# A two-layer diffusion trunk: the adaLN sums' start as a step of its own, their steps placed anew, and raw output weights loaded earlier

## The chip, the cores and the metric

One core of a Trainium2 chip. The metric is the device time of one execution, in microseconds (us). Five engines work at the same time, each through its own list of instructions in order: TensorE (PE, matmuls), VectorE (DVE), ScalarE (ACT), GpSimd (POOL) and SyncE (SP), which here only issues DMA transfers. POOL and ACT issue some DMAs too.

## What is computed

A trunk of two layers over 512 latent tokens and 256 context tokens of width 1024, all in float32. Cut to what matters:

```python
mod_lat = (silu_c @ ada_w[i] + ada_b[i])          # adaLN: 6 vectors of 1024
sh1, sc1, g1, sh2, sc2, g2 = jnp.split(mod_lat, 6, axis=-1)
h_lat = modulate(rmsnorm(x, norm_g[i, 0]), sh1, sc1)
y_lat = hybrid_na_sgu(...) if i % 2 == 0 else retention_mixer(...)
x = x + g1 * rmsnorm(y_lat, norm_g[i, 1])
h = modulate(rmsnorm(x, norm_g[i, 2]), sh2, sc2)
x = x + g2 * rmsnorm(conv_ffn(h, ...), norm_g[i, 3])
```

The same is done for the context tokens with their own vectors, except behind the retention of layer 1, whose output for the context isn't needed. Layer 0 mixes with neighbourhood attention beside spatial gating, layer 1 with retention in 8 heads. Both have a gated MLP (the ffn) of width 2816 with a depthwise convolution.

## The kernel before, in words

**Stages.** Spatial gating (until about 158 us), attention of layer 0 (until about 330), the first ffn (turns until about 890), retention (975 to 1445), the second ffn (1470 to 1850). Every float32 matmul is made of three: weights and data are split into a high and a low part. `split` (L110) lets ACT write the high part and DVE the low one. Raw weights come through `load` (L97), which issues on SP's queue, into one of only three buffers of the tag "raw" (512 KB each). These three serve ffn_in (f00.., f10..), ffn_out (fo..) and the adaLN weights (ar..). A smaller buffer ("rawu") takes the other half of ffn_in (f01.., f11..).

**The adaLN vectors.** `setup` makes four of layer 0's twelve half vectors at the start; each of the others is made by a generator, `ada_half` (L251), for half a vector of 512. It clears an accumulator `acc` for each stream with a memset on POOL (L257) and writes the bias into its first row by DMA (L258 in the code; the row is issued on POOL where `side` is set, otherwise on SP through `load`). Then it loads the weights in four parts and adds them up on DVE, 4 (two streams) or 2 operations for a part; each is an `acc<-ar,cs,acc` of 128x512. After each part it yields. At the end acc is split (ah, al). For gates (halves 4, 5, 10, 11) a matmul with ones sums over the partitions (ag), and the product with a row of norm_g is written (ngr, then G); for the last two of layer 0 it goes to DRAM (`away`, g<-ngr). For shifts and scales a matmul with `sel` (ac), a copy (arow) and a transpose (at) bring the sums into columns. There is one acc for each stream: the next half's memset waits for the split of the half before.

**Where the steps go.** `self.jobs` holds the generators that a stage has to finish, and `bg(n)` (L238) runs the next n steps of the first one; `bg_all` runs what is left. The calls of bg stand between the pieces of the main work: three among the projections of attention's first pair and one in every second turn of its loop of 42 (L872 and after); four held together in retention's head 0 and four in each later head (L1391 and after); one to four in each turn of an ffn (L1703 and after). Operations pass a scheduler that orders each engine's instructions by expected readiness, except those issued while `hold` is set, which keep the program's order. So a moved call moves what is near it too.

**Around the change.** Attention splits its keys (ka, kb) into halves of the partitions; kb's upper half is copied by POOL (L970). POOL also makes the bias tiles from a slab that it loads and scales (L991 to L1005). In an ffn each turn j has products of features with weights of turn j (wa, wb, wc, wd, split from f00 and f01), takes of PSUM into `pre`, and pieces of the output product of earlier pairs (wf), whose results go to yp or ypg and from there to DRAM by POOL's accumulating DMAs (L1688). `w_out` (L1653) loads and splits one ffn_out row block; it is called once a turn. The last two turns' features have their own end (`out_last`).

Of the kernel before, what the change touches and what calls it, by code (L numbers as in the profile page):

```python
# [13 lines left out]
ALU = mybir.AluOpType  # L14
AX = mybir.AxisListType

P = 128
# [7 lines left out]
NF = 22  # L25
# [53 lines left out]
class Trunk:  # L79
# [170 lines left out]

    def ada_half(self, l, half, streams, gate=None, away=False, fine=False, side=False):  # L251
        S, V, T, G = self.S, self.V, self.T, self.G
        m, h = divmod(half, 2)
        acc = []
        for s in range(streams):
            t = (self.lp if s else self.bp).tile([P, 512], F32, name=f"acc{l}{half}{s}", tag=f"acc{s}", bufs=1)
            G.memset(t, 0.0)  # L257
            (G.dma_start if side else self.load)(t[0:1], self.a["adab_row"][l * 12 + half : l * 12 + half + 1])  # L258
            acc.append(t)
        for kp in range(4):  # L260
            raw = self.bp.tile([P, 1024], F32, name=f"ar{l}{half}{kp}", tag="raw", bufs=3)
            self.load(raw, self.ada_unit_src(l, half, kp))
            for kk in range(2):
                k = kp * 2 + kk
                for s in range(streams):
                    V.scalar_tensor_tensor(
                        out=acc[s],
                        in0=raw[:, kk * 512 : kk * 512 + 512],
                        scalar=self.cs[:, 8 * s + k : 8 * s + k + 1],
                        in1=acc[s],  # L270
                        op0=ALU.mult,
                        op1=ALU.add,
                    )
                if fine and kk == 0:
                    yield
            yield
        sp = []
        for s in range(streams):
            hi = self.t2k(f"ah{l}{half}{s}", F32R)
            lo = self.t2k(f"al{l}{half}{s}", F32R)  # L280
            self.split(hi, lo, acc[s])
            sp.append((hi, lo))
            if fine:
                yield
            if m in (2, 5):
                ps = self.ps(f"ag{l}{half}{s}", "C")
                T.matmul(ps, self.ones, hi, start=True, stop=False)
                T.matmul(ps, self.ones, lo, start=False, stop=True)
                ngr = self.t2k(f"ngr{l}{half}{s}")
                row = l * 4 + (1 if m == 2 else 3)  # L290
                src = self.a["norm_g"][row : row + 1, h * 512 : h * 512 + 512].broadcast_to([P, 512])
                (G.dma_start if side else self.load)(ngr, src)
                dst = gate[s][:, h * 512 : h * 512 + 512]
                if away:
                    V.tensor_tensor(out=ngr, in0=ps, in1=ngr, op=ALU.mult)
                    G.dma_start(dst, ngr)
                else:
                    V.tensor_tensor(out=dst, in0=ps, in1=ngr, op=ALU.mult)
        if m in (2, 5):
            return  # L300
        ps = self.ps(f"ac{l}{half}", "C")
# [11 lines left out]
        for s in range(streams):  # L313
            if m in (0, 3):
                V.tensor_copy(ab[:, s, 1, h * 4 : h * 4 + 4], pt[:, :, s])
            else:
                V.scalar_tensor_tensor(
                    out=ab[:, s, 0, h * 4 : h * 4 + 4],
                    in0=pt[:, :, s],
# [538 lines left out]
    def attention(self, y, final):  # L858
        a = self.a
        with ExitStack() as ctx:  # L860
# [13 lines left out]
            fills = self.project_pair(0, pairs[0])  # L874
            for i, f in enumerate(fills):
                f()
                if i in (0, 2, 4):
                    self.bg()
            self.take_qk(0, pairs[0])
            fills = self.project_pair(1, pairs[1])  # L880
            toks = (4, 5, 0, 1, 2, 3)
            for i in range(n + lag):
# [26 lines left out]
                if i < n and step == 3:  # L909
                    self.take_v(j, pr)  # L910
                if i % 2:
                    self.bg()
            self.bg_all()
            for f in fills:
# [200 lines left out]
    def retention(self, y, final):  # L1115
        S, V, T, G, a = self.S, self.V, self.T, self.G, self.a
        KS = float(np.float32(P) ** np.float32(-0.5))
        with ExitStack() as ctx:
# [231 lines left out]
            for h in range(8):  # L1350
                vg_tiles(h)
                if h == 0:
# [15 lines left out]
                    for half in range(2):  # L1368
# [6 lines left out]
                        for n in (range(4) if half else (2, 0, 1, 3)):  # L1375
# [10 lines left out]
                            if half and n == 2:  # L1386
# [3 lines left out]
                                states(h)  # L1390
                    V.hold = True  # L1391
                    self.bg(4)
                    V.hold = False
                else:
# [15 lines left out]
                    for tp in (2, 0, 1):  # L1410
                        nat(h, wv, tp, "v")
                        if tp < 2:
                            score(h, tp)
                    self.bg()
                    wg = vg(h, 16, "g")
# [3 lines left out]
                    self.bg()  # L1419
                if h < 7:  # L1420
                    wk = qk(h + 1, 8, "k")
                else:
                    self.turn += 3
                    o6 = f, w_out(6)
                    self.bg_all()
# [13 lines left out]
    def ffn(self, l, y, final, gates=None):  # L1439
# [13 lines left out]
        with ExitStack() as ctx:  # L1453
# [37 lines left out]
            def raw(src, name, up=False):  # L1491
                if up:
                    t = fp.tile([P, 1024], F32, name=f"{name}r", tag="rawu", bufs=1)
                else:
                    t = self.bp.tile([P, 1024], F32, name=f"{name}r", tag="raw", bufs=3)
                self.load(t, src)
                return t
# [154 lines left out]

            def w_out(f, kind="o"):  # L1653
                u = slot(kind, f"fo{l}{f}", 0)
                r = (l * NF + f) * P
                self.split(u[0], u[1], raw(a["ffn_out"][r : r + P], f"fo{l}{f}"))
                return u
# [37 lines left out]
            def o(i):  # L1695
                for _ in range(per[i]):
                    if pieces:
                        pieces.pop(0)()
# [4 lines left out]
            for j in range(2, NF):  # L1703
# [5 lines left out]
                group = j // 2 * 2 - 2  # L1709
                feats = [gs.get(group + i) for i in range(GF)]  # L1710
                product(X, d[11], hb(11), "only")
                product(Y, d["s", 2], hb(("t", 1)), "only")
# [12 lines left out]
                step()  # L1725
                o(1)
                if j % 2 == 0 and group < LAST:
                    wo = nwo + [w_out(group + 1)]
                    pieces += out_steps(feats, wo, group)
# [6 lines left out]
                if j % 2 and j - 1 < LAST:  # L1736
                    nwo = [w_out(j - 1)]
                if first and j > 3:
# [6 lines left out]
                if j > 3:  # L1745
                    self.bg(2 if first and j > 5 and j % 2 else 1)
            while pieces:
# [55 lines left out]
    def build(self):  # L1803
# [26 lines left out]
        with ExitStack() as ctx:  # L1830
# [6 lines left out]
            g1 = self.gate_tiles(0, 1, 2)  # L1837
            self.jobs = [self.ada_half(0, h, 2, g1) for h in (4, 5)] + [self.ada_half(0, h, 2) for h in (6, 7, 8, 9)]
            self.sgu(y, xn)
# [4 lines left out]
            g2 = [self.dp.tile([P, D], F32, name=f"g2{s}", tag=f"g2{s}") for s in range(2)]  # L1844
            self.jobs = [self.ada_half(0, h, 2, list(g2), True, True, True) for h in (10, 11)]
            self.jobs += [self.ada_half(1, h, 2, fine=True, side=True) for h in range(4)]
            y = {}
# [5 lines left out]
        g3 = self.gate_tiles(1, 1, 1)  # L1853
        self.jobs = [self.ada_half(1, h, 1, g3 if h < 6 else None) for h in range(4, 10)]
        y = {}
# [5 lines left out]
        g4 = self.gate_tiles(1, 2, 1)  # L1861
        self.jobs = [self.ada_half(1, h, 1, g4, side=True) for h in (10, 11)]
        y = {}
# [111 lines left out]
```

## Time and profile before

| | |
|---|---|
| median of 3 runs | 1856.04 us (1852.79 to 1858.48) |
| the profiled execution | 1852.3 us, of which the span of instructions is 1850.5 us |
| granted TensorE clock, mean | 0.990 |
| DMA | 253.45 MB, 137 GB/s on average |
| POOL's DMA queue | 26912 packets, 51.95 MB |
| SP's and ACT's DMA queues | 55044 and 2304 packets |

How to read it: a row of a timeline has the start in the span, the duration, the engine, the line, the operation with its output and inputs, a count, and in brackets how long the engine stood idle before it and what ended that. A row of the list of waits has who waits for whom, total us, number of times and the longest. A row of the table of stretches has the stretch, its length, the busy time of PE, its weight loads, DVE, ACT and POOL (with counts), the granted clock, the share of DMA engines that are busy, and GB/s. Nearly all operations are recorded by one helper and so bear line 71; they are told apart by their tiles.

### The profile page before, as it was taken

The page shows a single profiled execution, that of the slowest core. Times are in us where ns is not written, and L with a number is a line of the kernel's source. Part 1 is how long each engine was busy: PE and PEld are TensorE (multiplying, and loading weights), DVE is VectorE, ACT ScalarE, POOL GpSimd, SP SyncE. Part 2 cuts the span into 40 slices and gives each one's busy share as a digit, 9 for nine tenths or more (in the row PEclk, how much of TensorE's full clock was granted, in tenths as well). Part 3 has the DMA queues.
Part 4 walks back from the last instruction along what each step waited for, and adds up shares of the span by engine and source line. Part 5 has one row for each costly group of instructions (what it writes and reads, how often), then busy time and mean ns, then how long its engine had stood idle before and what let it go on. Part 6 is the DMA issues. An engine that isn't in the chain of part 4 may idle for free. (4 is left out here: it accounts for less than half of the span.)

```text
span 1850.5 us, 28777 instructions
## 1 busy us (share of the span) xinstructions
PE 1781.8 (96%) x10928; PEld 1582.7 (86%) x10928; DVE 1391.1 (75%) x2347; ACT 1029.3 (56%) x1866; POOL 330.0 (18%) x462
## 2 busy tenths in 40 slices
PE   7999899999999999999999999999999889999997
PEld 4888777679998899998888988988999789989996
DVE  4877675789878788787866676676656699988886
ACT  6533455677555565564664534344434467766763
POOL 1102122131122322222112011011101100222221
PEclk9999999999999999999999999999999989999999
DMA  7344321155577777786722422331321225877762
GB/s 297 112 141 143 117 82 36 55 171 148 178 156 168 174 175 161 156 173 151 265 97 92 143 99 80 125 113 58 105 69 60 101 82 157 215 197 201 171 161 97
DMA packets 84399, 253.45 MB, mean 137 GB/s; under 512 B 11026, under 2 KB 11538, under 8 KB 84260
## 3 DMA queue, kind: packets, MB, share of 16 engines
q1 hardware_dynamic: 55044, 191.27, 30.9%
q0 software_dynamic: 26912, 51.95, 16.4%
q10 hardware_dynamic: 2304, 8.39, 1.1%
q8 instruction: 86, 1.41, 0.3%
q14 instruction: 53, 0.43, 0.1%
HBM read 191.80 MB, written 39.85 MB: 125 GB/s over the span
## 5 line engine op out<-in xcount | busy, mean ns | idle before, releaser
L71 DVE SCALAR_TENSOR_TENSOR acc<-ar,cs,acc 128x512 f32<-128x512 f32 x256 | 185.7, 751 | 33.7 <-DMA ar<-in_adaw 24.7
L71 DVE SCALAR_TENSOR_TENSOR cv<-pre,cw,cv 128x769 f32<-128x769 f32 (+1 forms) x176 | 153.6, 884 | 4.9 <-ACT cv L71 4.2
L71 PE MATMUL rn<-rwv,h0c 128*128 128x256 f32 x768 | 136.3, 281 | 3.0 <-ACT h0c L71 3.0
L71 PEld LDWEIGHTS rn<-rwv,h0c 128*128 128x128 f32 x768 | 118.2, 191 | 3.7 <-ACT h0c L71 3.4
L71 PE MATMUL wf<-fo,g 128*128 128x512 f32 x432 | 112.6, 394 | 0.5 <-DVE fo L71 0.5
L71 PE MATMUL rn<-rwv,h1c 128*128 128x256 f32 x384 | 108.1, 282 | 0.4 <-DVE h1c L71 0.2
L1688 POOL DMA_DIRECT2D yf<-yp x64 | 55.1, 861 | 257.0 <-ACT yp L71 233.8
L71 ACT ACTIVATE cv<-pre,cw 128x770 f32<-128x770 f32 (+1 forms) x88 | 81.3, 925 | 24.0 <-DVE pre L71 23.4
L71 PE MATMUL rn<-rwg,h0c 128*128 128x256 f32 x512 | 90.0, 280 | 0.0
L71 PEld LDWEIGHTS wf<-fo,g 128*128 128x128 f32 x432 | 75.9, 188 | 13.8 <-DVE fo L71 1.4
L71 PE MATMUL px<-hs,wc 128*128 128x384 f32 (+1 forms) x480 | 79.3, 314 | 5.4 <-ACT pre L71 3.2
L71 PEld LDWEIGHTS px<-hs,wc 128*128 128x128 f32 x480 | 74.3, 191 | 10.8 <-ACT pre L71 5.4
L71 ACT ACTIVATE pre<-px 128x256 f32<-128x256 f32 (+2 forms) x160 | 54.3, 367 | 47.7 <-PE px L71 47.6
L71 ACT COPY yp<-wf 128x512 f32<-128x512 f32 x118 | 67.8, 576 | 19.0 <-PE wf L71 16.5
L71 PEld LDWEIGHTS rn<-rwg,h0c 128*128 128x128 f32 x512 | 78.1, 189 | 0.0
L71 PE MATMUL pz<-hb,wa 128*128 128x384 f32 (+1 forms) x480 | 77.3, 308 | 0.0
L71 PE MATMUL px<-hb,wa 128*128 128x384 f32 (+1 forms) x480 | 77.1, 308 | 0.0
L71 PE MATMUL py<-blk,wb 128*128 128x384 f32 (+1 forms) x480 | 76.9, 308 | 0.0
L71 PE MATMUL px<-blk,wb 128*128 128x384 f32 (+1 forms) x480 | 76.7, 309 | 0.0
L71 PEld LDWEIGHTS px<-hb,wa 128*128 128x128 f32 x480 | 73.2, 188 | 3.2
L71 PEld LDWEIGHTS px<-blk,wb 128*128 128x128 f32 x480 | 73.4, 189 | 3.0 <-ACT pre L71 0.2
L71 PEld LDWEIGHTS rn<-rwv,h1c 128*128 128x128 f32 x384 | 72.9, 190 | 1.5 <-DVE h1c L71 1.3
(1272 smaller groups left out, 5112.6 us busy)
## 6 DMA issues: line engine op xcount, KB each, us to landing
ar<-in_adaw SPq DMA_DIRECT2D x96, 512.0 KB, 3.9
yf<-yp POOLq DMA_DIRECT2D x64, 256.0 KB, 4.2
yd<-yp POOLq DMA_DIRECT2D x54, 256.0 KB, 5.0
yd<-ypg POOLq DMA_DIRECT2D x54, 256.0 KB, 4.9
fin<-xd SPq DMA_DIRECT2D x8, 512.0 KB
xn<-in_x SPq DMA_DIRECT2D x6, 512.0 KB, 4.6
xb<-in_x SPq DMA_DIRECT2D x6, 512.0 KB
xd<-xb ACTq DMA_DIRECT2D x6, 512.0 KB, 2.8
```

The source lines that it names most:

```text
L71: i = f(*args, **kw)
L1688: G.dma_start((yd[t] if first else y[t])[:, o], v, accum_op=ALU.add)
```

## The change

- In `ada_half` the memset and the bias row become a step of their own, with a yield behind it, and the bias row is issued on POOL's queue always. 18 rows move there from SP's.
- That step is run ahead of time: for a stage's first half by `side_work` at the stage's start, for each later half by `prime` when the last split of the half before has been issued (not for halves that go to DRAM).
- Halves that go to DRAM form the gate's product in acc itself and store it from there; before, it was formed in ngr, a buffer of the t2k tag with four slots.
- `apart` adds a yield behind the split of gate halves in retention.
- Attention: the three calls of bg among the first projections are gone. In the loop bg is called from turn 5 on, in odd turns and in every eighth; the call at turn 5 is held in program order on DVE.
- Retention: in head 0 the weights of head 1's k are loaded first, and two unheld steps follow in place of four held ones. Later heads have five calls in place of four.
- The first ffn: one more call in each turn after the fifth, and the last call of a turn always runs one step (70 in place of 62; the steps to be run are 67 in place of 65).
- Both ffns: in turns 3 to 18 the raw output weights of the next `w_out` are loaded at the turn's start; the split stays where it was.

```diff
+    def prime(self):
+        if len(self.jobs) > 1:
+            next(self.jobs[1])
+    def side_work(self, jobs):
+        self.jobs = jobs
+        next(jobs[0])
...
             G.memset(t, 0.0)
-            (G.dma_start if side else self.load)(t[0:1], self.a["adab_row"][l * 12 + half : l * 12 + half + 1])
+            G.dma_start(t[0:1], self.a["adab_row"][l * 12 + half : l * 12 + half + 1])
             acc.append(t)
+        yield
...
             sp.append((hi, lo))
-            if fine:
+            if s == streams - 1 and not away:
+                self.prime()
+            if fine or apart and m in (2, 5):
                 yield
...
                 if away:
-                    V.tensor_tensor(out=ngr, in0=ps, in1=ngr, op=ALU.mult)
-                    G.dma_start(dst, ngr)
+                    V.tensor_tensor(out=acc[s], in0=ps, in1=ngr, op=ALU.mult)
+                    G.dma_start(dst, acc[s])
...
-            for i, f in enumerate(fills):
+            for f in fills:
                 f()
-                if i in (0, 2, 4):
-                    self.bg()
...
-                if i % 2:
+                if i > 4 and (i % 2 or i % 8 == 0):
+                    self.V.hold = i == 5
                     self.bg()
+                    self.V.hold = False
...
-                    V.hold = True
-                    self.bg(4)
-                    V.hold = False
+                    wk = qk(1, 8, "k")
+                    self.bg(2)
...
                         if tp < 2:
                             score(h, tp)
+                        if tp < 1:
+                            self.bg()
...
-                if h < 7:
+                if 0 < h < 7:
                     wk = qk(h + 1, 8, "k")
-                else:
+                elif h:
...
+            def w_raw(f):
+                r = (l * NF + f) * P
+                return raw(a["ffn_out"][r : r + P], f"fo{l}{f}")
-            def w_out(f, kind="o"):
+            def w_out(f, kind="o", ready=None):
                 u = slot(kind, f"fo{l}{f}", 0)
-                r = (l * NF + f) * P
-                self.split(u[0], u[1], raw(a["ffn_out"][r : r + P], f"fo{l}{f}"))
+                self.split(u[0], u[1], w_raw(f) if ready is None else ready)
...
+                f = j - 1 if j % 2 else group + 1
+                early = w_raw(f) if 2 < j and f < LAST + 1 - j % 2 else None
...
                 o(1)
+                if first and j > 5:
+                    self.bg()
...
-                    wo = nwo + [w_out(group + 1)]
+                    wo = nwo + [w_out(group + 1, ready=early)]
...
-                    nwo = [w_out(j - 1)]
+                    nwo = [w_out(j - 1, ready=early)]
...
                 if j > 3:
-                    self.bg(2 if first and j > 5 and j % 2 else 1)
+                    self.bg()
...
-            self.jobs = [self.ada_half(0, h, 2, list(g2), True, True, True) for h in (10, 11)]
-            self.jobs += [self.ada_half(1, h, 2, fine=True, side=True) for h in range(4)]
+            jobs = [self.ada_half(0, h, 2, list(g2), True, True, True) for h in (10, 11)]
+            self.side_work(jobs + [self.ada_half(1, h, 2, fine=True, side=True) for h in range(4)])
...
-        self.jobs = [self.ada_half(1, h, 1, g3 if h < 6 else None) for h in range(4, 10)]
+        self.side_work([self.ada_half(1, h, 1, g3 if h < 6 else None, apart=True) for h in range(4, 10)])
```

More of the change, by code (lines that the diff above doesn't have):

```diff
@@ L249, in bg_all, with ada_half @@
             self.bg()
-    def ada_half(self, l, half, streams, gate=None, away=False, fine=False, side=False):
+    def prime(self):
[4 more added lines that the diff above has]
+        next(jobs[0])
+    def ada_half(self, l, half, streams, gate=None, away=False, fine=False, side=False, apart=False):
         S, V, T, G = self.S, self.V, self.T, self.G
@@ L1837, in build @@
             g1 = self.gate_tiles(0, 1, 2)
-            self.jobs = [self.ada_half(0, h, 2, g1) for h in (4, 5)] + [self.ada_half(0, h, 2) for h in (6, 7, 8, 9)]
+            self.side_work([self.ada_half(0, h, 2, g1 if h < 6 else None) for h in (4, 5, 6, 7, 8, 9)])
             self.sgu(y, xn)
@@ L1861, in build @@
         g4 = self.gate_tiles(1, 2, 1)
-        self.jobs = [self.ada_half(1, h, 1, g4, side=True) for h in (10, 11)]
+        self.side_work([self.ada_half(1, h, 1, g4, side=True) for h in (10, 11)])
         y = {}
```

## The prediction

> **What bounds the kernel now.** I read the page first (busy time per engine), then the table of stretches, then the list of what TensorE (PE) waits for, and at each of those waits the timelines of the engines behind it.
>
> ```profile
> span 1850.5 us, 28777 instructions
> ...
> PE 1781.8 (96%) x10928; PEld 1582.7 (86%) x10928; DVE 1391.1 (75%) x2347; ACT 1029.3 (56%) x1866; POOL 330.0 (18%) x462
> ```
>
> PE stands still for only 1850.5 - 1781.8 = 68.7 us. No matmul is removed here, so whatever the change brings has to come out of these 68.7 us. The columns of the next view are the stretch, its length, and busy time by engine; of the list of waits: who waits for whom, total us, times, longest.
>
> ```profile
> 176.00:197.00 21.00, 13.90 (x65) 11.36 (x64) 13.77 (x20) 10.44 (x22) 10.35 (x10) 0.84 0.33 108
> 197.00:284.00 87.00, 86.08 (x510) 69.02 (x509) 66.42 (x174) 49.12 (x114) 19.01 (x29) 1.00 0.28 90
> 440.00:856.00 416.00, 411.72 (x2137) 379.84 (x2136) 337.77 (x481) 240.90 (x415) 99.83 (x130) 1.00 0.71 165
> ```
> ```profile
> PE s L71 <- POOL kb L970: 7.1, 1, 7.1
> ...
> PE rt L71 <- DVE rg L71: 2.8, 2, 1.6
> PE at L71 <- ACT arow L71: 2.4, 1, 2.4
> ...
> PE wf L71 <- DVE fo09l L71: 1.8, 1, 1.8
> PE rkc L71 <- ACT rwk L71: 1.7, 1, 1.7
> PE ag L71 <- ACT ah L71: 1.3, 2, 1.2
> PE wsg L71 <- ACT wos L71: 1.1, 2, 0.9
> ...
> PE rkc L71 <- DVE rwk L71: 0.3, 1, 0.3
> ```
>
> The reader is to see that PE is the bound nearly everywhere (86.08 of 87, 411.72 of 416), and that the waits are few. These, and the two in the fences below (1.64 and 1.16), add up to 7.1 + 2.8 + 2.4 + 1.8 + 1.7 + 1.3 + 1.1 + 1.6 + 1.2 = 21 us. That is the ceiling of what the change can win: 1.1%. What it can lose has no such ceiling.
>
> **The change part by part.** I give each place as a change of PE's idle time: the value I take, and both ends in brackets.
>
> *Attention's start, the largest.*
>
> ```profile
> 180.91 0.40 PE L71 MATMUL ac<-ah,sel 128*2 128x512 f32 x1
> ...
> 181.84 0.28 PE L71 MATMUL py<-h0a,wv 128*128 128x256 f32 x1
> ...
> 192.07 0.58 PE L71 MATMUL s<-kb,q 128*128 128x256 f32 x1 [7.10 <-POOL kb L970]
> ```
> ```profile
> 184.04 0.40 POOL L998 TENSOR_SCALAR slab<-slab 128x256 f32<-128x256 f32 x1 [2.66 <-DMA slab<-in_rpb]
> 184.50 0.98 POOL L257 MEMSET acc<- 128x512 f32 x2
> 190.09 1.93 POOL L970 CAST kb<-kb 64x768 fp32r<-64x768 f32 x1 [4.61 <-DVE kb L71]
> ```
> ```profile
> 185.40 0.33 SPq L97 DMA_DIRECT2D ar<-in_adaw  x1
> ```
> ```profile
> 188.75 0.75 DVE L71 SCALAR_TENSOR_TENSOR acc<-ar,cs,acc 128x512 f32<-128x512 f32 x1 [5.63 <-DMA ar<-in_adaw]
> ```
>
> VectorE (DVE) works in order. Its first sum of half 8 waited 5.63 us for a weight load that SP could issue only at 185.40, behind the bias row, which waited for the memset of 184.50; the pieces of kb, queued behind the sum, were late, and PE with them. The changed program has no sum there: the three early steps are gone and the loop starts stepping after i = 4. Then the copy of kb waits for POOL itself, which has the slab until 184.04 + 0.40 = 184.44, and ends 1.93 later, at 186.4 instead of 190.09 + 1.93 = 192.0: 5.6 us sooner. The four matmuls of half 7 (180.91 to 181.84, 0.9 us) and its transpose, some 0.3, move from in front of this wait to behind it: they filled it and now cost their time. **-4.4** (-5.6 if they find another gap; -3 if POOL or ACT delays kb by another 1.4). What is late next is POOL's slab.
>
> *The rest of attention.* Eight sums of 0.75 us (6 us of DVE) and their splits move into the loop, where PE idles 0.92 us in 87 and DVE 20.6: cover enough on average, but in-order DVE delays softmax pieces behind a sum. **+0.5** (0 to +2).
>
> *Spatial gating.* The bias rows no longer stand in SP's queue ahead of the wos weights. **-0.5** of that row's 0.9 (-0.9 to 0).
>
> *The first ffn, halves 10 and 11 and the half after.*
>
> ```profile
> 552.42 0.75 DVE L71 SCALAR_TENSOR_TENSOR acc<-ar,cs,acc 128x512 f32<-128x512 f32 x1 [2.07 <-DMA acc<-in_adab_row]
> ...
> 563.00 0.69 DVE L71 TENSOR_TENSOR s<-f008r,f018r 128x512 f32<-128x512 f32 x1 [4.17 <-issue]
> ```
> ```profile
> 559.09 0.52 POOL L258 DMA_DIRECT2D acc<-in_adab_row  x1
> ```
> ```profile
> 571.77 0.50 PE L71 MATMUL wf<-fo04h,g 128*128 128x512 f32 x1 [1.64 <-ACT ypg L71]
> ```
> ```profile
> g<-ngr POOLq DMA_DIRECT2D x4, 256.0 KB, 4.7
> ```
> ```profile
> L97 SPq DMA_DIRECT2D acc<-in_adab_row x18: 231/244/298, 51.9 to 1311.8; - x18
> L258 POOL DMA_DIRECT2D acc<-in_adab_row x14: 504/526/859, 284.6 to 1621.0; - x14
> ...
> DMA to landing us min/median/max: 1.7/3.9/6.1
> ```
>
> Before, DVE stood 2.07 us for a bias row and 4.17 for a t2k buffer whose gate product was still being stored (the store of g takes 4.7 to land); PE lost 1.64 us here and 1.8 at fo09l, the same pattern one half later. In the changed kernel the product lies in acc and is stored from there, so t2k comes free. But the next half's memset must now wait for that store (4.7), then its bias row follows on the same POOL queue (3.9 to land), and the stores of yp are queued behind both. The memset is issued a step ahead; with 65 steps in these 416 us a step is 6.4 us, so some 2.2 of the 8.6 stay in sight, against 2.07 + 4.17 before. DVE has 78 us free in 416. I take **-0.8 at each of the two, -1.6** (-3.4 if both waits go; +2 if the chain on POOL costs as much again as it frees).
>
> [...]
>
> *The first ffn's end.* Eight more calls are spread over the turns, so half 2 of layer 1 ends a turn earlier and at<-arow (2.4) has twelve more matmuls between itself and its ac; **-2.4** (-2.4 to -1).
>
> *Retention's start.* In the changed order the weights of head 1's k are loaded ahead of the sums, and only two unheld steps follow.
>
> ```profile
> 998.05 1.06 ACT L71 ACTIVATE rwk<-rwk1r 128x1024 fp32r<-128x1024 f32 x1 [1.32 <-DMA rwk1r<-in_ret_qk]
> ```
> ```profile
> 1010.59 1.22 DVE L71 TENSOR_TENSOR rwo<-rwo00r,rwo 128x1024 fp32r<-128x1024 f32 x1
> ```
>
> Waits that go: rkc 1.7 and its tail 0.3, and half of the 1.6 at rt, 2.8 in all. What comes: two DVE splits of 1.22 (rwk1, rwo01) stand ahead of the rv and kd pieces that PE needs at its state matmuls, 2.4 us. That leaves -0.4 up to head 1's q; behind it both waits at ag (1.3) go, since that half ends later, inside a head: **-1.7** (-4.5 if the splits find room and all of rt goes, +1 if the stall at the states is that of a load, 3.9 to land as adaLN's, instead of 1.2).
>
> *Retention, head 6.*
>
> ```profile
> 1325.91 0.75 DVE L71 SCALAR_TENSOR_TENSOR acc<-ar,cs,acc 128x512 f32<-128x512 f32 x1 [1.48 <-DMA ar<-in_adaw]
> ```
>
> This sum, ahead of head 5's outputs, is what made the second rt wait (2.8 - 1.6 = 1.2). With five steps a head the halves end earlier and it isn't there: **-1.0** (-1.2 to 0).
>
> *The second ffn.* The raw output weights now take the raw buffer that comes free first, so the next ffn_in load waits for the split before.
>
> ```profile
> 1584.86 0.33 SPq L97 DMA_DIRECT2D f108r<-in_ffn_in  x1
> ```
> ```profile
> 1586.91 1.23 DVE L71 TENSOR_TENSOR fo<-fo15r,fo 128x1024 fp32r<-128x1024 f32 x1
> ```
> ```profile
> 1591.91 0.36 ACT L71 ACTIVATE pre<-px 128x256 f32<-128x256 f32 x1
> ...
> 1638.84 1.06 ACT L71 ACTIVATE wa<-f1011r 128x1024 fp32r<-128x1024 f32 x1 [4.88 <-DMA f1011r<-in_ffn_in]
> ```
> ```profile
> 1595.73 1.63 PE L71 MATMUL px<-hs,wc 128*128 128x256 f32 x12
> ...
> 1644.07 1.63 PE L71 MATMUL px<-hs,wc 128*128 128x256 f32 x12 [1.16 <-ACT pre L71]
> ```
>
> f108r goes from 1584.86 to the end of fo15's split, 1588.14: 3.3 us later. ACT's wa stands before pre<-px, whose result PE needs at 1595.73; pre ended at 1592.27, so there is 3.5 us of slack. In turn 11, where ACT waited 4.88 for such a load, PE lost 1.16. So 3.3 later just fits, and in the changed order pre<-px stands ahead of wa in this turn. **+0.5** (-1 to +3).
>
> **Sum.** -4.4 + 0.5 - 0.5 - 1.6 - 2.4 - 1.7 - 1.0 + 0.5 = **-10.6 us**. All lower ends: -19; all upper ends: +4. The profiled execution took 1852.3 us (1.8 around its span) and becomes 1841.7; it stands 3.7 below the median of the runs, 1856.0, which becomes **1845 us** (0.6% less).
>
> **The rivals.**
>
> 1. *POOL takes SP's place.* The kb copy behind the slab (-3 instead of -4.4), the memset behind g's store (+2 instead of -1.6) and the two splits ahead of rv (0 instead of -1.7) give back 1.4 + 3.6 + 1.7 = 6.7: -3.9, so **1852**, no change. For it: the store and the row are 4.7 and 3.9 us on one queue, and POOL copies 1.93 us just where PE waits. Against: a step of lead, and POOL 18% busy. [...] That the moved steps do nothing at all (1856) I hold for 3 in 100, since their places in the instruction order do change.
> 2. *Slower: the raw buffers run dry.* Three buffers serve ffn_in, ffn_out and adaLN loads. One is now held half a pair longer in turns 3 to 18 of each ffn. If each of these 16 turns of the second ffn waits as turn 11 did (1.16), that is +18.6 instead of +0.5: -10.6 + 18.1 = +7.5, so **1864**. It decides once an ffn_in load is more than 3.5 us later than now. For it: the 3.3 us above, and a queue where loads wait in order. Against: 3.3 is still under 3.5, and in turn 8 the new order places wa behind pre.
>
> **How the numbers follow.** A measurement of this kernel can tell about 0.3% (5.6 us) from no change. The forecast, faster by more than that, gets 0.60; rival 1 with no effect at all 0.24; slower 0.16, of which rival 2 has 0.12. The range goes from all lower ends (1856.0 - 19, rounded down to 1836) to all upper ends (1860); 0.04 lie below, 0.14 above.
>
> **What would show it.** After: the kb wait of PE near 185 is 1 to 3 us instead of 7.10, and DVE has no 5.63 us gap before it; at<-arow, rkc<-rwk and ag<-ah leave the list of PE's waits; the gaps at ypg and fo09l are under 1 us each; DVE's waits for bias rows on POOL are no longer than 2.07; f108r is issued near the end of fo15's split. I am wrong if PE's idle time in 176 to 197 stays above 5 us, if new waits px<-pre or wf<-fo of over 1 us recur from turn to turn in an ffn, or if POOL's memset after g's store holds up acc for more than 4 us.

## The result, and the profile after

The changed kernel takes 1858.45 us (median of 20 runs, 1851.14 to 1867.24) beside 1851.28 us for the kernel before (20 runs, 1845.54 to 1858.48): a ratio of 1.0037, with a 95% interval from 1.0024 to 1.0050. It is slower by some 7 us, where 10.6 us less had been predicted.

The page of the kernel after, busy time per engine:

```profile
span 1857.4 us, 28752 instructions
...
PE 1787.2 (96%) x10928; PEld 1586.3 (85%) x10928; DVE 1389.9 (75%) x2347; ACT 1028.5 (55%) x1866; POOL 339.2 (18%) x480
```

The span grew by 6.9 us. PE runs the same 10928 matmuls and stands still for 1857.4 - 1787.2 = 70.2 us, against 68.7 before. So the waits that went were paid back almost exactly by others, and 5.4 us more are counted as busy: 2.9 in gating (where PE also begins 1.2 us sooner), 2.9 in the gate halves, 2.0 in retention and -1.9 in attention make up most of it. The list of what PE waits for in the kernel after (who for whom, total us, times, longest) shows which they are:

```profile
PE px L71 <- DVE pre L71: 4.7, 3, 2.7
...
PE px L71 <- ACT pre L71: 4.0, 6, 1.5
PE wf L71 <- DVE fo09l L71: 3.9, 1, 3.9
...
PE ug L71 <- DVE un L71: 2.3, 1, 2.3
...
PE s L71 <- POOL kb L982: 1.0, 1, 1.0
```

The wait for kb fell from 7.1 to 1.0, and at<-arow, rkc<-rwk and ag are gone, as forecast. New are px<-DVE pre (0.4 before), ug<-un, and more of fo09l (1.8 before) and of px<-ACT pre (3.2 before).

For the place of the loss I cut both traces at the first starts of the same matmuls. The table of stretches has, of the kernel after, gating without its first 25 us, attention, the gate halves of the first ffn, and the second ffn; then the same of the kernel before (columns as in the prediction):

```profile
25.00:162.10 137.10, 132.31 (x753) 105.57 (x753) 101.02 (x178) 62.91 (x108) 12.21 (x24) 0.99 0.42 145
162.10:397.87 235.77, 223.95 (x1250) 174.60 (x1249) 168.18 (x407) 137.66 (x317) 65.24 (x88) 1.00 0.29 92
...
542.64:695.70 153.06, 144.78 (x729) 132.96 (x729) 117.44 (x168) 81.98 (x142) 41.36 (x54) 0.97 0.74 164
...
1450.52:1825.38 374.86, 357.06 (x2446) 326.62 (x2445) 323.62 (x520) 250.43 (x461) 67.65 (x87) 0.99 0.60 158
```
```profile
25.00:158.13 133.13, 130.62 (x752) 103.97 (x753) 101.11 (x178) 62.89 (x109) 9.15 (x18) 1.00 0.44 150
158.13:397.36 239.23, 225.87 (x1250) 175.78 (x1249) 169.82 (x407) 137.15 (x317) 61.44 (x84) 0.99 0.28 90
...
541.14:686.38 145.24, 141.84 (x729) 131.19 (x729) 116.84 (x167) 82.45 (x143) 40.01 (x52) 0.99 0.76 175
...
1448.99:1818.95 369.96, 356.77 (x2445) 328.37 (x2444) 323.04 (x519) 250.70 (x461) 67.37 (x87) 0.98 0.61 160
```

| stage | before, us | after, us | difference | predicted |
|---|---|---|---|---|
| gating, from 0 | 158.13 | 162.10 | +4.0 | -0.5 |
| attention | 239.23 | 235.77 | -3.5 | -3.9 |
| first ffn up to the gate halves | 143.78 | 144.77 | +1.0 | 0 |
| first ffn, gate halves and the turns behind | 145.24 | 153.06 | +7.8 | -1.6 |
| rest of the first ffn and its end | 217.85 | 212.84 | -5.0 | -2.4 |
| retention | 544.76 | 541.98 | -2.8 | -2.7 |
| second ffn | 369.96 | 374.86 | +4.9 | +0.5 |

The sum is +6.4. Three stages lose 16.7 us that the prediction had at -1.6; three gain 11.3 where it had 9.0. In the gate halves 2.9 of the 7.8 are busy time at a mean clock of 0.97 in place of 0.99; in the second ffn nearly all is idle time (374.86 - 357.06 = 17.8 against 13.2).

**Gating.** The timeline of the kernel after, where it leaves before:

```profile
96.11 0.53 POOL L266 MEMSET acc<- 128x512 f32 x1 [9.97 <-DVE al L71]
96.93 0.58 POOL L267 DMA_DIRECT2D acc<-in_adab_row  x1 [0.29 <-POOL acc L266]
100.02 0.75 DVE L71 SCALAR_TENSOR_TENSOR acc<-ar,cs,acc 128x512 f32<-128x512 f32 x1 [3.96 <-DMA acc<-in_adab_row]
100.69 1.66 DVE L71 SCALAR_TENSOR_TENSOR un<-mx,sgub,un 128x384 f32<-128x384 f32 x3
101.35 0.51 PE L71 MATMUL ug<-ug,h0a 128*128 128x256 f32 x2 [2.27 <-DVE un L71]
```

In the kernel before, DVE did the pieces of un first and the sum after them:

```profile
97.74 2.19 DVE L71 SCALAR_TENSOR_TENSOR un<-mx,sgub,un 128x384 f32<-128x384 f32 x4 [1.53 <-PE mx L71]
```

The changed order puts the sum ahead of un. It waits 3.96 us for its bias row, and the main work behind it waits too.

**The gate halves.** The timeline of the kernel after:

```profile
567.06 0.53 POOL L266 MEMSET acc<- 128x512 f32 x1 [4.40 <-DMA g<-acc]
567.88 0.54 POOL L267 DMA_DIRECT2D acc<-in_adab_row  x1 [0.30 <-POOL acc L266]
571.00 0.75 DVE L71 SCALAR_TENSOR_TENSOR acc<-ar,cs,acc 128x512 f32<-128x512 f32 x1 [3.68 <-DMA acc<-in_adab_row]
571.67 0.55 DVE L71 TENSOR_TENSOR pre<-pre,px 128x384 f32<-128x384 f32 x1
572.27 2.96 PE L71 MATMUL px<-hs,wd 128*128 128x384 f32 x12 [2.73 <-DVE pre L71]
...
640.87 0.33 SPq L97 DMA_DIRECT2D ar<-in_adaw  x1
647.29 0.75 DVE L71 SCALAR_TENSOR_TENSOR acc<-ar,cs,acc 128x512 f32<-128x512 f32 x1 [3.91 <-DMA ar<-in_adaw]
647.96 1.22 DVE L71 TENSOR_TENSOR fo09l<-fo09r,fo09h 128x1024 fp32r<-128x1024 f32 x1
```

This is read as a chain: POOL waits 4.40 us for the store of g out of acc, then clears acc and issues the row; DVE stands 3.68 for the row with `pre` behind it in its queue; PE stands 2.73 for pre. At 647 it is a weight load in place of a row. It goes out at 640.87, when the sums before it have ended (638.64 + 2.20 = 640.84) and, as I read it, have freed a raw buffer; it holds a sum that stands ahead of the split of fo09, and PE waits 3.9.

**The second ffn.** The kernel before issues the load of f107r ahead of that of fo15r:

```profile
1572.17 0.33 SPq L97 DMA_DIRECT2D f107r<-in_ffn_in  x1
1574.88 0.33 SPq L97 DMA_DIRECT2D fo15r<-in_ffn_out  x1
```

In the kernel after the order is turned round (this stage begins 1.5 us later there). Its timeline:

```profile
1575.31 0.33 SPq L97 DMA_DIRECT2D fo15r<-in_ffn_out  x1
1577.94 0.33 SPq L97 DMA_DIRECT2D f107r<-in_ffn_in  x1
...
1584.90 1.06 ACT L71 ACTIVATE wa<-f107r 128x1024 fp32r<-128x1024 f32 x1 [4.06 <-DMA f107r<-in_ffn_in]
1584.90 0.69 DVE L71 TENSOR_TENSOR s<-f107r,f117r 128x512 f32<-128x512 f32 x1 [2.41 <-DMA f107r<-in_ffn_in]
...
1587.68 1.65 PE L71 MATMUL px<-blk,wb 128*128 128x256 f32 x12 [1.53 <-ACT pre L71]
...
1591.86 1.22 DVE L71 TENSOR_TENSOR fo<-fo15r,fo 128x1024 fp32r<-128x1024 f32 x1
1592.01 0.33 SPq L97 DMA_DIRECT2D fo16r<-in_ffn_out  x1
1593.11 0.33 SPq L97 DMA_DIRECT2D f108r<-in_ffn_in  x1
```

f107r goes out 5.8 us later than before, and the wait for it holds ACT for 4.06 us and DVE for 2.41. A turn later the same comes again: fo16 is loaded early and holds a buffer, and f108r goes out as soon as the split of fo15 has ended (1591.86 + 1.22 = 1593.08).

### The profile page after: what moved, and what is told of

It reads as the page before. It is cut to its first block, busy times and chain, and to the rows that moved or that the text cites. A ratio compares the mean times of both kernels' runs of the same rounds, so it can differ in the third digit from the quotient of the medians.

```text
span 1857.4 us, 28752 instructions
## 1 busy us (share of the span) xinstructions
PE 1787.2 (96%) x10928; PEld 1586.3 (85%) x10928; DVE 1389.9 (75%) x2347; ACT 1028.5 (55%) x1866; POOL 339.2 (18%) x480
## 5 line engine op out<-in xcount | busy, mean ns | idle before, releaser
L71 PEld LDWEIGHTS px<-hs,wc 128*128 128x128 f32 x480 | 73.4, 190 | 10.6 <-ACT pre L71 5.3
```

Source lines behind the costliest of these rows:

```text
L71: i = f(*args, **kw)
```

## The experiments

My theory after the result: three parts cost, each at one place. (1) The bias rows on POOL's queue, and the gates stored out of acc, put DMA waits in front of DVE's main work. (2) The raw weights loaded early let the three raw buffers run dry. (3) The new places of the steps gain. The rivals: the new places themselves cost, through fuller turns of the first ffn; or the own step costs, whatever its queue.

Times and ratios are against the kernel before, run on the same chip at the same time; it took 1857.8 to 1858.8 us there, and 1851.3 beside the kernel after, so ratios are compared and not times. The trace of before stems from an execution of 1852.3 us, so the experiments' stages read against it come out too long, for most kernels by 4 to 10 us over the whole (from -2 in e11 to 10 in e2). I use such stages only where they set kernels apart. A stage of one trace also varies where nothing in it was changed: the gate halves have the same order of instructions on all five engines in the kernel after, e1 and e4, and are 7.8, 13.6 and 13.6 us longer there than in before. So a few us in one stage of one trace prove little; the ratios decide.

| kernel | us | ratio to before | 95% interval |
|---|---|---|---|
| e1: rows on SP | 1866.70 | 1.0040 | 1.0026 to 1.0054 |
| e2: gates out of ngr | 1859.24 | 1.0015 | 0.9997 to 1.0032 |
| e3: no early raw weights | 1857.50 | 0.9996 | 0.9985 to 1.0007 |
| e4: attention's places as before | 1869.19 | 1.0054 | 1.0035 to 1.0073 |
| e5: e1, e2 and e3 together | 1854.79 | 0.9977 | 0.9966 to 0.9989 |
| e6: before, with early raw weights alone | 1867.80 | 1.0052 | 1.0036 to 1.0069 |
| e7: before, with all new places alone | 1854.07 | 0.9977 | 0.9964 to 0.9990 |
| e8: e7 without the first ffn's | 1850.25 | 0.9957 | 0.9940 to 0.9974 |
| e9: before, with the own step alone | 1883.18 | 1.0127 | 1.0106 to 1.0148 |
| e10: e8 with three late calls | 1850.49 | 0.9959 | 0.9944 to 0.9974 |
| e11: e9 with e1 and e2 | 1878.04 | 1.0104 | 1.0082 to 1.0127 |
| e12: e5 with the first rows on POOL | 1851.85 | 0.9967 | 0.9956 to 0.9979 |

**e1, the rows' queue.**

```diff
-            G.dma_start(t[0:1], self.a["adab_row"][...])
+            (G.dma_start if side else self.load)(t[0:1], self.a["adab_row"][...])
```

> The changed kernel, but the 18 bias rows that it moved to POOL's queue are issued on SP's queue again; the step of its own stays. Theory (each stage loses by its own new wait): in spatial gating the first sum of half 5 stood ahead of the four un pieces on DVE and waited 3.96 us for a bias row on POOL's queue; PE lost 2.27 us and then ran at half clock for some 4 us, 4.0 us in all between 75 and 110. In this kernel's order that sum stands behind the un pieces, so the stretch comes back to before's length: -4 us there, nothing in the ffns, about 1854.5 in all. Rival (the loss lies in the step of its own, the queue doesn't matter): the row behind a memset on POOL is late on either queue, another sum waits, and the stretch keeps at least 3 of the 4 us.

1.0040, no different from the kernel after. The stall in gating is gone: PE loses only 0.2 us against before between 75 and 115 us, where the kernel after loses 4.2. But 5.0 us are lost in the first 25 us. The timeline of e1:

```profile
3.53 0.61 SPq L97 DMA_DIRECT2D acc<-in_adab_row  x2
...
14.48 0.75 DVE L71 TENSOR_SCALAR xn<-xn,x00r 128x1024 f32<-128x1024 f32 x1 [4.23 <-POOL x00r L341]
19.59 0.75 DVE L71 TENSOR_SCALAR xn<-xn,x01r 128x1024 f32<-128x1024 f32 x1 [4.36 <-POOL x01r L341]
```

The first half's step is now run ahead of time, and so its two rows stand among the first loads of x on SP. In the kernel after, DVE does these two pieces at 12.44 and 14.04. POOL's queue was right for the first rows and wrong for the next ones.

**e2, the gates' store.**

```diff
-                    V.tensor_tensor(out=acc[s], in0=ps, in1=ngr, op=ALU.mult)
-                    G.dma_start(dst, acc[s])
+                    V.tensor_tensor(out=ngr, in0=ps, in1=ngr, op=ALU.mult)
+                    G.dma_start(dst, ngr)
```

> The changed kernel, but the gate products of layer 0's last two halves are formed in and stored from ngr again, so the next memset of acc doesn't wait for the store. Theory (the chain store, memset, bias row on POOL's queue is what costs 7.8 us between 550 and 660): the waits of 3.7 us for the bias row at 571 and PE's 2.73, 0.96 and 3.85 go, with the half clock behind them; the stretch becomes 4 to 8 us shorter, about 1852 in all. Rival (the buffers of t2k run out again and DVE stands for the store as in the kernel before, 4.17 us): the stretch is as long as before's or longer, PE waits of 1.5 to 2 us at ypg and fo09l, at most 4 us won.

1.0015: the store out of acc is worth about 0.2%, though the two intervals overlap. In the trace the stretch from 540 to 590 us costs 0.8 us against before, in the kernel after 5.0, and PE's wait at px<-hs,wd is 1.30 in place of 2.73. The memset no longer waits for a store. The whole stretch of the gate halves is still 4.7 us longer than in before.

**e3, the early raw weights, taken out.**

```diff
-                early = w_raw(f) if 2 < j and f < LAST + 1 - j % 2 else None
+                early = None
```

> The changed kernel without the early loads of raw output weights: w_out loads and splits at the same place again, in both ffns. Theory (raw buffers: an ffn_in load waits for the split of the output weights before it): in the second ffn the PE waits of 1.53, 1.52, 0.77 and 1.21 us (1586 to 1706) go and before's 1.16, 0.47 and 0.60 come back; 4 to 5 us shorter between 1570 and 1720; the first ffn hardly changes (1 us). About 1853.5 in all. Rival (the second ffn's loss comes from the adaLN sums of its two halves, now with a memset and row of their own): the stretch stays within 1.5 us of the changed kernel's.

0.9996: the early load costs 0.41%, 7.6 us, as much as the change loses in all. The second ffn's length falls back to that of before (+0.01 us in the trace, +4.9 after); where the rest of the 7.6 lies, the traces don't show.

**e4, attention's places put back**, as in the removed lines of the diff.

```diff
+                if i in (0, 2, 4):
+                    self.bg()
...
-                if i > 4 and (i % 2 or i % 8 == 0):
-                    self.V.hold = i == 5
+                if i % 2:
                     self.bg()
-                    self.V.hold = False
```

> The changed kernel with the bg calls of attention where they were before (three among the first projections, one in every second turn). Theory (the early sums cost the 7.1 us wait for kb and the half clock behind it, the late ones cost the softmax): PE's wait at s<-kb is 6 us or more again, the stretch 175 to 200 is 8 to 10 us longer, and 200 to 350 5 to 6 us shorter; in all 3 us slower than the changed kernel, about 1861. Rival (with the memset ahead of time the first sum finds its weights loaded, and the kb wait stays short with the sums in their old place): the wait is under 3 us, the rest of attention is short too, and the kernel is 4 us or more faster than the changed one.

1.0054, 0.17% above the kernel after with intervals that overlap. The list of waits of e4 shows the stall back, and attention is 0.3 us longer than before in place of 3.5 shorter:

```profile
PE s L71 <- POOL kb L982: 7.7, 1, 7.7
```

**e5, the three undone together.** The edits of e1, e2 and e3.

> The changed kernel with three parts undone at once: the 18 rows on SP's queue, gate products in ngr, raw output weights loaded late. What stays is the step of its own and the new places of the steps. Theory (these three carry all of the loss, and the places win what was forecast): the changed kernel's ratio to the kernel before was 1.0037; minus 7.6 us for the late loads, 4 for the gate, 2 to 4 for the rows in spatial gating gives 0.996 (0.994 to 0.998). Rival (the losses overlap, all of them wait for the same DMA queues, and a wait taken away uncovers the next): 0.999 to 1.001, as with the late loads alone (0.9996).

0.9977, clearly faster than before: without the three the loss is a gain. It still has e1's late start, +4.5 us in gating, and the gate halves are still 9.2 us longer than in before, with a wait of 8.4 at fo09l. So what these turns lose doesn't go with the three.

**e6, the early raw weights alone**, in the kernel before.

```diff
+                early = w_raw(f) if 2 < j and f < LAST + 1 - j % 2 else None
...
-                    nwo = [w_out(j - 1)]
+                    nwo = [w_out(j - 1, ready=early)]
```

> The kernel before with one part of the change alone: raw output weights loaded at the turn's start. Theory (an ffn_in load behind the split of the output weights is late whatever the sums do): in the second ffn PE gets waits of 1 to 3 us at four places or so, 5 to 8 us in all, 1.003 to 1.004. Rival (it hurts only together with the adaLN steps moved into the ffns' turns): within 0.1%.

1.0052: 9.7 us by itself, no less than in company. The timeline of e6 shows the mechanism at its plainest:

```profile
1674.26 1.22 DVE L71 TENSOR_TENSOR fo<-fo110r,fo 128x1024 fp32r<-128x1024 f32 x1
1675.51 0.33 SPq L97 DMA_DIRECT2D f1013r<-in_ffn_in  x1
...
1682.71 0.69 DVE L71 TENSOR_TENSOR s<-f1013r,f1113r 128x512 f32<-128x512 f32 x1 [3.04 <-DMA f1013r<-in_ffn_in]
...
1683.78 2.10 PE L71 MATMUL px<-hs 128*128 128x256 f32 x12 [2.98 <-DVE pre L71]
```

f1013r goes out when the split of fo110 ends (1674.26 + 1.22 = 1675.48). ACT waits for it too (3.50 us, at wa), but what PE waits for is DVE: the sum of the weights s<-f10 stands ahead of pre in its queue. The kernels with the early load spend 4.9 to 8.6 us more in the second ffn than before (after, e1, e2, e4, e6); the eight without it between -0.7 and +3.4. The early load with a buffer of its own was not tried.

**e7 and e8, the places alone.** e7 is the kernel before with the new calls of bg in attention, retention and the first ffn; e8 leaves out the first ffn's.

```diff
                 o(1)
-                if first and j > 5:
-                    self.bg()
...
-                    self.bg()
+                    self.bg(2 if first and j > 5 and j % 2 else 1)
```

> The kernel before with the new places of the steps in attention, retention and the first ffn, and nothing else: no step of its own, no rows moved, no early loads. Theory (the places are what wins: attention -3.9, retention -3, the first ffn's end -3.7 as the traces of the changed kernel show): -8 to -11 us, 0.994 to 0.996. Rival (without a memset ahead of time, the sums in their new places wait for memset and row): 0.998 to 1.000.

> As the kernel with the new places alone, but the first ffn's calls stay as before. Theory: attention -3.9 and retention -3 without the first ffn's end: 0.996 to 0.9975. Rival (more calls in the first ffn push sums against loads there and cost as much as its end wins): as fast as or faster than with all places.

0.9977 and 0.9957. e8 is the fastest of all, 0.43% below the kernel before, and beats both kernels with an edit of attention and retention alone. In its trace the kb wait is 0.9 us, attention 4.2 and retention 2.7 us shorter than before. The first ffn's fuller turns, taken by themselves, win nothing: from e8 to e7 the stretch with the gate halves grows from +1.1 to +6.1 us (ag<-al 2.18 and fo09l 3.32 appear), and the rest shrinks from +1.1 to -1.5 (at<-arow goes). One trace each would be weak evidence, but the others agree: without the store out of acc, the gate halves cost 4.7 to 9.2 us in the four kernels with the fuller turns (e2, e5, e7, e12), and 1.1 and -0.9 in the two that have before's calls in these turns and no own step (e8, e10).

**e9 and e11, the own step alone.** e9 is the kernel before with prime, side_work and the new `ada_half`, at the old calls; e11 is e9 with rows and gates by the old queue and buffer (the edits of e1 and e2). Both have the yields of `apart`.

> The kernel before with the step of its own alone: memset and bias row ahead of time, all rows on POOL's queue, gate products of layer 0's last two halves in acc; all calls of bg and all loads as before. Theory (this part loses where the sums stand ahead of needed work on DVE and wait for a row from POOL): spatial gating +4 us as in the changed kernel (first sum of half 5 ahead of the un pieces), the first ffn's halves between 550 and 660 +4 to +8; 1.003 to 1.006. Rival (the new places make these waits; with the old places a row a step ahead is always in time): 0.998 to 1.001, the kb wait at 185 shorter than 7.1 us.

> As the kernel with the step of its own alone, but rows on SP's queue where they were and the gate products in ngr: only the separate step and its being run ahead remain. Theory (queue and store make the cost, not the step): spatial gating and the first ffn within 2 us of the kernel before, 0.999 to 1.001. Rival (the step ahead of time costs by itself, since a memset waits on POOL with other work behind it): 1.002 or more.

1.0127 and 1.0104, the slowest of all. The list of waits of e9:

```profile
PE rt L71 <- DVE rg L71: 7.8, 4, 3.7
...
PE htc L71 <- DVE fin L71: 5.2, 2, 4.4
```

Each half has one step more, and two of the first ffn's six halves are not run ahead by `side_work` or `prime`: 67 steps meet 62 calls, so five are left over, in place of three, and run at its end, where fin waits. In retention, where `apart` adds two steps, the sums slip to where head outputs are formed (rt), and this stage alone grows by 16.7 us in e9 and 11.0 in e11. In gating e9 has the stall of the kernel after (PE waits 2.2 us at ug<-un; the stage is only 0.5 us longer than in before, being 1.3 ahead at 25 us), and e11, with the rows on SP, hasn't. In the gate halves, at before's calls, the store out of acc and the rows show by themselves: +8.5 in e9, +2.7 in e11. So the step and the calls belong together. Added up, the parts alone would give +1.27 + 0.52 - 0.23 = +1.56%; together they give +0.37%. With the new calls in place the own step costs e3 less e7, 0.19% (with intervals that overlap a little), and not 1.27%. As far as the intervals can tell, all of this goes with its queue and its store: e5 has the step without them, and is at 0.9977 as e7 is. By e9 less e11 they are 0.23%, with intervals that overlap.

**e10, three more calls at the first ffn's end**, to win at<-arow for e8 as well.

```diff
-                    self.bg(2 if first and j > 5 and j % 2 else 1)
+                    self.bg(2 if first and j > 5 and (j % 2 or j > 15) else 1)
```

> The kernel with the new places of attention and retention alone (0.9957), and three more steps in turns 16, 18 and 20 of the first ffn, so that its steps end before its last turns. Theory (spread over all turns the extra calls put sums among the gate halves, where DVE waits; late ones only take the 2.4 us wait at at<-arow away): another 2 to 4 us, 0.9935 to 0.995. Rival (the wait at<-arow comes from ACT's order and moves with the step): the same as without, 0.9957, with an at<-arow wait somewhere else.

0.9959, the same as e8. at<-arow is gone from the waits, but the timeline has another:

```profile
874.31 1.06 ACT L71 ACTIVATE fo019h<-fo019r 128x1024 fp32r<-128x1024 f32 x1 [5.64 <-DMA fo019r<-in_ffn_out]
875.40 1.23 DVE L71 TENSOR_TENSOR fo019l<-fo019r,fo019h 128x1024 fp32r<-128x1024 f32 x1 [3.57 <-ACT fo019h L71]
878.35 1.97 PE L71 MATMUL px<-hs,wd 128*128 128x384 f32 x5 [5.53 <-DVE pre L71]
```

The wait of 2.4 us is gone and one of 5.5 has come: fo019 arrives late. The steps' weight loads share the raw buffers with it, which I take for the cause; it was not tried apart.

**e12, the first rows on POOL, the others on SP**, in e5.

```diff
-            G.dma_start(t[0:1], self.a["adab_row"][...])
+            (G.dma_start if side or (l, half) == (0, 4) else self.load)(t[0:1], ...)
```

> The kernel with three parts undone, but the two bias rows of the very first half are issued on POOL's queue (as the changed kernel does); the other rows stay on SP's. Theory (run ahead of time, those two rows stand on SP's queue among the first loads of x: in both kernels with rows on SP the second x load is issued 1.6 to 2.1 us later and DVE waits 4 us twice for it, which is the 5 us lost in the first 25 us): the start comes back to before's, within 1 us, spatial gating stays without the 4 us wait, and the whole goes from 0.9977 to about 0.995. Rival (the first 25 us vary from run to run with the transfers of x, whatever the rows do): the start is 3 to 5 us late again, the whole 0.9977.

0.9967. DVE has un ahead of the sum again, and gating is 0.7 us shorter than before, where e5's was 4.5 longer. The timeline of e12:

```profile
97.63 2.19 DVE L71 SCALAR_TENSOR_TENSOR un<-mx,sgub,un 128x384 f32<-128x384 f32 x4 [1.81 <-PE mx L71]
99.74 3.11 DVE L71 SCALAR_TENSOR_TENSOR acc<-ar,cs,acc 128x512 f32<-128x512 f32 x4
```

That settles the gating stage. Of the 5 us, the median shows 0.1%, within the intervals; in the trace the second ffn is 3.4 us longer than in before, where e5's was 0.2 longer: ACT waits 6.04 us for a load of fo110 and PE 2.04 for pre behind it; why that load is late there stays open. The first gate half, from 540 to 590 us, gains 1.7 us against before (0.3 in e5, with the same order there), where 0.8 had been predicted for the changed kernel; then PE waits 6.0 us at fo09l in e12 too, so that wait is of the fuller turns and not of the store.

## Why the prediction was wrong, step by step

**Right in size, in part by luck: attention.** -3.9 predicted, -3.5 measured, and +0.3 with the places put back (e4). The kb wait fell to 1.0, below the 1 to 3 forecast. But two terms were off, and the errors cancel. From the matmul that starts at 181.84 in before to the one at 196.72, the kernel after wins 8.2 us, where 5.6 had been forecast: with the wait of 7.1 the clock of 0.50 from 190.07 to 196.90 went as well, which the sum did not have. The rest of attention gives 5.3 back, where 0.5 and 1.2 for the moved matmuls had been forecast; PE waits there for sc, ptall and vt (1.9, 1.7 and 1.1 us), which it did not in before or not as long. Of the 3.5 in all, 239.23 - 225.87 - (235.77 - 223.95) = 1.5 are idle time; 1.9 are matmuls that no longer run at the lower clock.

**Right in sign: retention and the first ffn's end.** The waits named, rkc, ag and at, are gone. In retention -2.7 against -2.8 is again a cancelling: idle time fell by 4.7, since the waits that come at the state matmuls are 1.2 us in place of 2.4 and rt falls from 2.8 to 0.6; busy time grew by 2.0, and why stays open. At the first ffn's end -5.0 stands against -2.4: beside at<-arow, 1.8 us of small waits at px and wf went, which the sum did not have.

**Wrong: "Spatial gating, -0.5".** It was +4.0. The step failed at "the bias rows no longer stand in SP's queue ahead of the wos weights": it priced the queue that the rows leave, and not who stands behind the sum that waits for them on the queue they come to. In before the sums came behind un; in the changed order one comes in front. That the row's queue makes this wait is shown: with the rows on SP it is gone (e1, e11, e12), with the rows on POOL it is there (after, e9).

**Wrong: the gate halves, "-0.8 at each of the two, -1.6".** It was +7.8. Two steps failed. The first is "some 2.2 of the 8.6 stay in sight": the chain on POOL that was named there and as rival 1 stays in sight in full, the store's 4.4 and the row's 3.7, since the lead of a step isn't there while the memset waits. Without the store (e2) 4.2 us between 540 and 590 go. The second is that more calls in these turns were priced only with what they win at the ffn's end, and at nothing here. Without the store the fuller turns still cost 4.7 to 9.2 us (e2, e5, e7, e12), with a wait of 3.3 to 8.4 at fo09l that I read as one for a raw buffer. The upper end, +2, also left out that PE would run slower behind the stall (2.9 us). How the 7.8 divide between the two stays open.

**Wrong in size: "The second ffn, +0.5 (-1 to +3)".** +4.9, and 0.41% by e3, 0.52% by e6. The step that failed followed one load, f108r, as 3.3 us late. It went out 8.3 us later (1593.11 against 1584.86), since f107r, a turn before, was late already: 5.8 us, behind the load of fo15, with a wait of 4.06 on ACT and 1.53 on PE. And the slack of 3.5 us was worked out on ACT's order alone (wa ahead of pre). DVE also has s<-f10 ahead of pre, and in turns 13 and 15 the late load costs PE 0.77 and 1.21 us there, in e6 2.98. Rival 2 was right in its mechanism and its sign; its price of 18.6 was too high, as a few of the 16 turns stall and not all.

**What this does to the sum.** Early raw weights +7.6 (0.41%) in place of +0.5; everything else about 0 (e3: 0.9996, from -2.8 to +1.3 us) in place of -11.1, of which the new places alone hold -4.3 (e7), with the first ffn's left as before -8 (e8), and the own step with its queue and store gives 3.5 back (e3 less e7).

## What to carry to other kernels

A wait taken off one queue is priced by what stands behind the waiting instruction in the order it will then have, on every engine that reads the late data, and not by the spare time of the engine that is named first. Where few buffers serve several streams, a load put earlier can make another one late (here, with three buffers, f107r by 5.8 us): count the buffers before the transfers. A step added to a background job needs a call added to its schedule, and parts that are bad or good alone (+1.27%, +0.52%, -0.23%) do not add up.

## What the runs showed of the hardware that had not been expected

A stall of PE can cost more than its length, by what the clock does behind it. The traces of before and after have the granted clock at 1.00 or at 0.50 and at nothing between; means such as 0.97 come from stretches that hold both. From 16 us on, all changes of the clock, 11 in before and 13 in after, lie in each trace on one grid of 3.41 us, and every stretch at 0.50 but the one at the very end is 3.41 or 6.83 us long. Behind the 2.73 us wait at 572.27 in the kernel after it is two cells of the grid:

```profile
573.77:580.60 6.83, 5.87 (x17) 4.79 (x17) 5.56 (x9) 4.16 (x9) 1.76 (x2) 0.50 0.65 138
```

So up to 0.50 x 6.83 = 3.4 us are lost beside the wait. It isn't a matter of the wait's length alone. In the kernel before, PE waited 1.77 us up to 639.72, at fo09l, and 2.37 up to 860.38, at at<-arow. The cells around the two are

```profile
637.21:640.63 3.42, 1.65 (x8) 1.03 (x7) 3.42 (x5) 1.08 (x3) 0.00 (x0) 1.00 0.57 159
640.63:644.04 3.41, 3.41 (x11) 2.92 (x10) 3.41 (x7) 2.64 (x4) 1.21 (x2) 0.50 0.88 208
...
855.67:859.08 3.41, 1.91 (x8) 1.05 (x6) 3.41 (x6) 2.61 (x6) 1.74 (x2) 1.00 0.35 35
859.08:862.49 3.41, 2.11 (x14) 2.09 (x15) 3.41 (x6) 3.41 (x8) 0.35 (x1) 1.00 0.84 158
862.49:865.90 3.41, 3.41 (x20) 3.27 (x19) 3.38 (x7) 1.92 (x5) 0.51 (x1) 1.00 0.92 192
```

The shorter wait lies in one cell, which leaves PE 1.65 us of work, and the clock is 0.50 in the next. The longer one falls into two cells, with 1.91 and 2.11 us of work, and the clock stays at 1.00. In these two traces, from 30 us on, a cell at full clock with at most 1.65 us of work was followed by one at 0.50 every time (12 cells), one with more than 1.8 never; of the five between, 1.68 to 1.77 us, one was.

Over the span the losses balance here: the stretches at 0.50, without the one at the very end, come to 30.7 us before and 30.7 after, so at most 15.4 us each. They decide single stages, not this result. In e9 the mean clock is 0.982 over a span of 1881.6 us, in before 0.990 over 1850.5: 0.018 x 1881.6 - 0.010 x 1850.5 = 15.4, so up to some 15 us more than in before are the clock's there.
